# Two pads that move where the on-chip tiles of a decoder block begin

## The chip, the core and the metric

The kernel runs on one core of a Trainium2 chip. The metric is the device time of one execution in microseconds (us); the time before is the median of three runs, 918.95 us (918.89 to 918.98). Engines are named as in the profile: PE is TensorE's matmul side, PEld its weight loads, DVE is VectorE, ACT is ScalarE, POOL is GpSimd, SP is the engine that issues most DMAs.

## What is computed

A decoder block on 512 tokens of width 1024, all in float32. Cut to its products:

```python
u = rmsnorm(x, norm_mix_g)
p = u @ w_in + b_in                      # 1024 -> 7424 columns, split in nine parts
y_attn = sliding_window_sink_attention(aq, ak, av, sinks)   # 16 heads, window 128
y_hgrn = hgrn2_branch(hq, hf, hi, hg, lb, hgrn_norm_g)      # 8 heads, chunks of 64
h = x + (sigmoid(gate_a) * (y_attn @ w_branch_attn)
         + sigmoid(gate_b) * (y_hgrn @ w_branch_hgrn)) @ w_out
u2 = rmsnorm(h, norm_ffn_g)
z = silu(u2 @ w_gate) * (u2 @ w_up)      # 2816 wide
out = rmsnorm(h + z @ w_down, norm_final_g)
```

## The kernel before, in words

[...] Each operand is split into a high part `h`, rounded to float32r, and a low part `l`, the rest; the three products hh, hl and lh are summed in PSUM. So a product of a 128-row block needs three matmuls, each with a weight load of its own.

Weights come from DRAM in units of 1 MB (`raw`, two buffers, class `Weights`), and are cut into granules of half a unit. ACT writes a granule's `wh` (L96) and DVE its `wl` (L100), 128 x 1024 each, three buffers of each, two granules ahead of use. A granule is used by 24 matmuls.

The stages, in the order of TensorE's work, which is the order of the program text:

- x is normalized, transposed and split into `uh` and `ul` (up to about 30 us).
- A stream of projections from `uh`, `ul` (`mm3`, L357 to L359, into `ps_big`: the weights are loaded into the array, 512 columns of `uh` or `ul` move). Attention per head group (`sc`, `pt`, `pv`) and then HGRN per head (`pa`, `pc`, `pk`, `pu`, `po`, `pot`) are put in between, in slots of 8 matmuls. The HGRN values (`ps_v`, `mm3n`, L367 to L369) have it the other way round: a block of `uh` is loaded, 256 columns of `wh` or `wl` move.
- The branch products: `ps_big` with `yh`, `yl` moving (attention's output, beside the last HGRN heads), and with `oh`, `ol` moving (HGRN's output), the latter in turn with four pairs of gate projections from `uh`, `ul`.
- The output projection (`ps_o`, `mm3n`): blocks of `mh`, `ml` are loaded, 256 columns of weights move.
- FFN gate and up (`ps_f`, `mm3`): weights are loaded, 512 columns of `u2h` or `u2l` move. POOL, ACT and DVE make `zh`, `zl` from it.
- Down projection (`acc`, L865): blocks of `zh`, `zl` are loaded, 512 columns of `wh` or `wl` move. Then the last rmsnorm and the stores.

On-chip memory has an address per partition. Pools stand on two stacks: pools of side "left" are put one above the other from the bottom, pools of side "right" one below the other from the top (`newpool`, L141). Where a pool begins thus follows from the sizes of those before it. The first on the left is `cst`, the constants, 8,896 bytes a partition, which begins at byte 16,512; `w`, with the weight buffers, begins right above it. On the right nothing stands below the first pool's top at byte 229,344. The bytes at which the operands of the matmuls begin, as the program places them:

| tiles | side | first byte | modulo 512 |
|---|---|---|---|
| `raw`, `wh`, `wl` (all buffers) | left | 25,408 to 62,272 | 320 |
| `uh`, `ul` | left | 66,368, 82,752 | 320 |
| `u2h`, `u2l` | left | 82,752, 101,184 | 320 |
| `zh`, `zl` | right | 139,232, 184,288 | 480 |
| `oh`, `ol` | right | 151,520, 167,904 | 480 |
| `yh` and `mh`, `yl` and `ml` | right | 196,576, 212,960 | 480 |
| `khh`, `kll`, `qst` (attention) | right | 116,384 and up | 160 |
| `ident` | left | 16,512 | 128 |

Slices of these tiles that one matmul reads begin a multiple of 512 bytes further on, so the last column holds for every matmul. The highest left tile that lives beside the lowest right tile, `m1` in the pool `gates`, ends at 115,520; `khh0` begins at 116,384, 864 bytes above it. Later pools use again what earlier ones of the other side left free: `of`, `u2l` and `diag` on the left, and attention tiles, `zg`, `sgf`, `gfin` and `yo` on the right, share bytes in this way.

Of the kernel before, what the change touches and what calls it, by code (L numbers as in the profile page):

```python
"""Hybrid decoder block: sliding-window GQA attention with sinks, HGRN2 gated
linear recurrence, sigmoid-gated merge, SwiGLU FFN, final rmsnorm.

Every product with a weight matrix runs in single-pass fp32r: an operand is
split exactly into h (rounded to fp32r) and l = x - h, and the products hh, hl
and lh are summed in fp32 in PSUM.
"""
# [1 line left out]

# [6 lines left out]
F32 = mybir.dt.float32  # L16
# [6 lines left out]
P = 128  # L23
# [11 lines left out]
WARM = 28  # L35
AHEAD = 2


class Weights:
    """Streams weights: 1 MB units from DRAM, cut into granules split in h, l."""  # L40

    def __init__(self, nc, pool, units):
        self.nc, self.pool = nc, pool
# [22 lines left out]
        self.raw[u] = t  # L66

    def load_half(self, u, half):
        """A column half of a unit of kind c, for an early start."""
        kind, w, c0 = self.units[u]  # L70
        if u not in self.raw:
            self.raw[u] = self.pool.tile([P, 2048], F32, tag="raw", bufs=2, name=f"raw{u}")
        self.nc.sync.dma_start(
            self.raw[u].rearrange("p (k n) -> p k n", k=KD)[:, :, half * P:half * P + P],
            w[:, c0 + half * P:c0 + half * P + P].rearrange("(k p) n -> p k n", p=P))
# [38 lines left out]
def block_kernel(ctx: ExitStack, tc: tile.TileContext, x, norm_mix_g, w_in, b_in,  # L114
# [6 lines left out]
    def raw_ins(ins):  # L121
        return getattr(ins, "ins", ins)

    def act(out_, in_, func, **kw):
        """An activation; those that need a table keep the order given here."""
        if func not in (AF.Sigmoid, AF.Exp, AF.Ln):
            return nc.scalar.activation(out_, in_, func, **kw)
        if tables["last"] is None:
            ins = nc.scalar.activation(out_, in_, func, **kw)
        else:  # L130
            with tc.issue_after(tables["last"]):
                ins = nc.scalar.activation(out_, in_, func, **kw)  # L132
        tables["last"] = raw_ins(ins)
        return ins
# [6 lines left out]
    def newpool(name, side, space=None):  # L141
        kw = dict(space=space) if space is not None else {}
        kw["reuse_waits"] = "tile"
        return tc.alloc_tile_pool(name=name, bufs=1, side=side, **kw)

# [1 line left out]
    units = [("c", w_in, C_K), ("c", w_in, 0)]  # L147
    for p in range(1, 4):
        units += [("c", w_in, 256 * p), ("c", w_in, C_GA + 256 * (p - 1))]
# [14 lines left out]
    units += [("f", w_d, 2 * p) for p in range(NF // 2)]  # L164

    cst = newpool("cst", "left")
    wpool = newpool("w", "left")
    upool = newpool("u", "left")
    W = Weights(nc, wpool, units)

# [1 line left out]
    ident = cst.tile([P, P], F32, name="ident")  # L172
    make_identity(nc, ident)
    ones = cst.tile([P, P], F32, name="ones")
# [12 lines left out]
    low_m = low.bitcast(U32).unsqueeze(1).broadcast_to([P, NT, P])  # L187
    up_m = up.bitcast(U32).unsqueeze(1).broadcast_to([P, NT, P])

# [1 line left out]
    spool = newpool("start", "right")  # L191
    psum = newpool("ps", "left", bass.MemoryType.PSUM)

# [6 lines left out]
    def psb(shape, name):  # L200
        return psum.tile(shape, F32, tag="big", bufs=3, name=name)

    xt = spool.tile([P, NT, D], F32, name="xt")
    rows = spool.tile([90, P], F32, name="rows")
# [21 lines left out]
    sinks = cst.tile([P, 16], F32, name="sinks")  # L226
# [1 line left out]
    hib = cst.tile([P, D], F32, name="hib")  # L228
    nc.sync.dma_start(hib, b_in[0:1, C_HI:C_HI + D].broadcast_to([P, D]))

    # the tensor engine's clock is released by activity: keep it busy till x is there
    pg = psb([P, P], "pg")
    for _ in range(WARM):
        pe.transpose(pg, ident, ident)
# [93 lines left out]
    yh = ypool.tile([P, KD, S], F32R, tag="h", name="yh")  # L328
    yl = ypool.tile([P, KD, S], F32R, tag="l", name="yl")

    # lower bounds: softmax over the two rows of logits, first row
    lb = cst.tile([P, 8], F32, name="lb")
    omlb = cst.tile([P, 8], F32, name="omlb")
    nhfb = cst.tile([P, 8], F32, name="nhfb")
# [15 lines left out]
    def bias(col):  # L350
        return prm[:, col // P:col // P + 1]

# [1 line left out]
    def mm3(ps, wh, wl, ah, al):  # L354
        """ps = w^T a, w stationary."""
        for k in range(KD):
            pe.matmul(ps, wh[:, k, :], ah[:, k, :], start=k == 0, stop=False)  # L357
            pe.matmul(ps, wh[:, k, :], al[:, k, :], start=False, stop=False)  # L358
            pe.matmul(ps, wl[:, k, :], ah[:, k, :], start=False, stop=k == KD - 1)  # L359
            if k in (2, 5):  # L360
                yield

    def mm3n(ps, ah, al, t, wh, wl, k0, first, last):
        """ps (+)= a[:, t]^T w over 4 K-blocks, a stationary."""
        ts = slice(t * P, (t + 1) * P)
        for k in range(4):
            pe.matmul(ps, ah[:, k0 + k, ts], wh[:, k, :], start=first and k == 0, stop=False)  # L367
            pe.matmul(ps, ah[:, k0 + k, ts], wl[:, k, :], start=False, stop=False)  # L368
            pe.matmul(ps, al[:, k0 + k, ts], wh[:, k, :], start=False,  # L369
                      stop=last and k == 3)  # L370
# [5 lines left out]
        evac(ps)  # L376
        yield

# [1 line left out]
    khh = [ap.tile([P, S], F32R, name=f"khh{g}") for g in range(2)]  # L380
    kll = [ap.tile([P, S], F32R, name=f"kll{g}") for g in range(2)]
    vhl = [ap.tile([P, NT, P], F32R, name=f"vhl{g}") for g in range(2)]
# [118 lines left out]
            act(yh[:, ks, :], yq, AF.Copy)  # L501
            tt(yl[:, ks, :], yq, yh.bitcast(F32)[:, ks, :], ALU.subtract)

# [1 line left out]
    pools = {}  # L505

    def open_hgrn():
# [8 lines left out]
    def v8(z):  # L516
        return z.rearrange("p (n c) -> p n c", c=64)

    def v42(z):
        return z.rearrange("p (s two c) -> p s two c", two=2, c=64)  # L520
# [4 lines left out]
    def T(tag, shape=(P, S), bufs=1, pool=None):  # L525
        return (pool or pools["h"]).tile(list(shape), F32, tag=tag, bufs=bufs, name=tag)
# [44 lines left out]
    def hgrn_prep(hd):  # L571
        z = hd_state[hd]
        sn, g, q = z["sn"], z["lf"], z["q"]
        om = omlb[:, hd:hd + 1]
        b = g
        dve.tensor_tensor_scan(b, reset, g, 0.0, ALU.mult, ALU.add)
        b8 = v8(b)
        d = T("d")
        tt(v8(d), b8, b8[:, :, 31:32].broadcast_to([P, 8, 64]), ALU.subtract)
        e = T("e", bufs=2)  # L580
        tt(v8(e), b8[:, :, 63:64].broadcast_to([P, 8, 64]), b8, ALU.subtract)
        E1, E2 = T("E1", bufs=2), T("E2", bufs=2)
        act(E1, d, AF.Exp)
        act(E2, d, AF.Exp, scale=-1.0)
        act(e, e, AF.Exp)
        EB = b
        act(EB, b, AF.Exp)
        dec = T("dec", (P, 8), 2)
        dve.tensor_copy(dec, v8(EB)[:, :, 63])
        dec2 = T("dec2", (P, NT), 2)  # L590
        d42 = dec.rearrange("p (s two) -> p s two", two=2)
        tt(dec2, d42[:, :, 0], d42[:, :, 1], ALU.mult)
        tt(E1, q, E1, ALU.mult)
        stt(E2, sn, om, E2, ALU.mult, ALU.mult)
        # intra-chunk on the diagonal, chunk 1 against chunk 0 of a pair beside it
        K0 = T("K0", (P, NT, 64), 2)
        QE1 = T("QE1", (P, NT, 64), 2)
        KS, QS = e, EB
        stt(K0, v42(sn)[:, :, 0, :], om, v42(e)[:, :, 0, :], ALU.mult, ALU.mult)
        stt(v42(KS)[:, :, 1, :], v42(sn)[:, :, 1, :], om, v42(e)[:, :, 1, :],  # L600
            ALU.mult, ALU.mult)
        tt(v42(KS)[:, :, 0, :], K0, d42[:, :, 1:2].broadcast_to([P, NT, 64]), ALU.mult)
        tt(QE1, v42(q)[:, :, 1, :], v42(EB)[:, :, 1, :], ALU.mult)
        tt(v42(QS)[:, :, 0, :], v42(q)[:, :, 0, :], v42(EB)[:, :, 0, :], ALU.mult)
        tt(v42(QS)[:, :, 1, :], QE1, d42[:, :, 0:1].broadcast_to([P, NT, 64]), ALU.mult)
        z.update(E1=E1, E2=E2, K0=K0, QE1=QE1, KS=KS, QS=QS, dec2=dec2)
# [40 lines left out]
    def hgrn_outputs(hd):  # L647
        z = hd_state[hd]
        A = pools["aT"][hd % 2]
        po = ps1([P, NT, P], "po")  # L650
        for s in range(NT):
            pe.matmul(po[:, s, :], A[:, s, :], z["v"][:, s, :], start=True, stop=s == 0)  # L652
            if s:
                pe.matmul(po[:, s, :], z["QS"][:, s * P:(s + 1) * P], z["st"][:, s - 1, :],
                          start=False, stop=True)
        # rmsnorm over the head's values
        sq = z["sq"] = T("sq", (P, NT, P))
        act(sq, po, AF.Square)
        ss4, r4 = T("ss4", (P, NT), 2), T("r4", (P, NT), 2)
        dve.tensor_reduce(ss4, sq, AX.X, ALU.add)  # L660
        rms_scale(r4, ss4, P, ss4)
        tt(sq, po, r4.unsqueeze(2).broadcast_to([P, NT, P]), ALU.mult)
# [6 lines left out]
        stt(pools["of"][:, hd, :], pt.rearrange("p s c -> p (s c)"), g_hn[:, hd:hd + 1],  # L669
            z["sg"], ALU.mult, ALU.mult)  # L670

# [1 line left out]
    def evac_ya(j):  # L673
        def go(ps):
            tt(m1[:, j, :], ps, m1[:, j, :], ALU.mult)
# [21 lines left out]
    beside = {}  # L697
# [31 lines left out]
    h1.release()  # L729
    h0.release()  # L730

# [1 line left out]
    mp = newpool("m", "right")  # L733
    ohlp = newpool("ohl", "right")
    oh = ohlp.tile([P, KD, S], F32R, name="oh")
# [38 lines left out]
    gpool.release()  # L774
    upool.release()

# [1 line left out]
    hpool = newpool("hn", "left")  # L778
    u2pool = newpool("u2", "left")
    rp = newpool("r", "right")  # L780
# [31 lines left out]
    rp.release()  # L812
    ypool.release()

# [1 line left out]
    zpool = newpool("z", "right")  # L816
    fp = newpool("f", "right")
    zh = zpool.tile([P, NF, S], F32R, name="zh")
# [10 lines left out]
    for p in range(NF // 2):  # L829
        gs = []  # L830
        for a in range(2):
            zg = fp.tile([P, S], F32, tag="zg", bufs=2, name="zg")
            first = p == 0 and a == 0
# [13 lines left out]
    fp.release()  # L847
    u2pool.release()

# [1 line left out]
    wd = newpool("wd", "left")  # L851
    dp = newpool("d", "right")
    gfin = dp.tile([P, D], F32, name="gfin")
# [19 lines left out]
    first = len(W.grans) - TAIL_F  # L873
    for i in range(first, len(W.grans)):
        W.split(i, wd, TAIL_F)
    for t in range(NT):
# [29 lines left out]
        stt(y[:, S + 256:D], y[:, S + 256:D], r1, gfin[:, S + 256:D], ALU.mult, ALU.mult)  # L906
        for q, hs in ((nc.scalar, slice(0, S)), (nc.sync, slice(S, D))):
            q.dma_start(out2[t * P:(t + 1) * P, hs], y[:, hs])
    for pl in (dp, zpool):
        pl.release()  # L910
    for pl in (wd, hpool, wpool, cst):
        pl.release()
# [31 lines left out]
```

## Time and profile before

| | |
|---|---|
| median of three runs | 918.95 us |
| span of the profiled execution | 917.3 us |
| instructions in the span | 11601 |
| PE busy | 905.9 us, 99% |
| PEld busy | 770.1 us, 84% |
| DVE, ACT, POOL busy | 463.2, 371.1, 142.8 us |
| HBM traffic | 82.90 MB read, 2.10 MB written |

The span runs from the first to the last instruction of the profiled execution; the device time holds the launch and the end around it too. A matmul's duration in the profile runs from its start to the modelled end of its drain, and two or three matmuls overlap; so durations of matmuls don't add up to time. The step from one start to the next does. In the timeline the first column is the start in us.

### The profile page before, as it was taken

To read this page: it belongs to the slowest core of one execution; us is meant where nothing else is said; L and a number is where in the kernel's file an instruction comes from. 1 tells how busy PE (TensorE), PEld (TensorE's weight loads), DVE (VectorE), ACT (ScalarE), POOL (GpSimd) and SP (SyncE) were. 2 spreads that over 40 slices of the span, in tenths; PEclk is the share of its full clock that TensorE was granted. 3 is DMA by queue.
4 is the path that set the end of the run, shared out by engine and by line. 5 is a ranking of instruction groups with operands and counts; after the bars stand their busy time and mean duration, and the time that the engine had idled before them with its cause. 6 is when DMAs were issued, how large, how long until landed. Compare 5 with 4: busy or idle time off the path is not lost.

```text
span 917.3 us, 11601 instructions
## 1 busy us (share of the span) xinstructions
PE 905.9 (99%) x4668; PEld 770.1 (84%) x4668; DVE 463.2 (50%) x725; ACT 371.1 (40%) x634; POOL 142.8 (16%) x148
## 2 busy tenths in 40 slices
PE   8999999999999999999999999999999999999996
PEld 7988889898888988888888998888888888888885
DVE  5677877647484855645345444344433443322314
ACT  5566765655452636125332443233222322211214
POOL 3004533300000000000000003222332233000004
PEclk9999999999999999999999999999999999999999
DMA  8231211323222141322252322222233332322212
GB/s 255 93 93 46 93 47 46 93 91 94 90 92 57 38 137 46 108 76 93 92 179 96 93 92 92 92 93 92 91 97 110 112 96 91 115 92 92 91 46 93
DMA packets 73522, 85.74 MB, mean 93 GB/s; under 512 B 1690, under 2 KB 68348, under 8 KB 73468
## 3 DMA queue, kind: packets, MB, share of 16 engines
q1 hardware_dynamic: 72876, 83.95, 28.7%
q10 hardware_dynamic: 592, 1.05, 0.3%
q8 instruction: 37, 0.61, 0.3%
q14 instruction: 17, 0.14, 0.0%
HBM read 82.90 MB, written 2.10 MB: 93 GB/s over the span
## 4 chain that ended last, share of the span: by engine, by line
PE 97%; SPq 1%; DMA 0%; POOL 0%; DVE 0%; issue 0%; ACT 0%; POOLq 0%; DVEq 0%
PE acc L865 13%; PE ps_big L358 13%; PE ps_big L359 13%; PE ps_big L357 13%; PE ps_f L357 9%; PE ps_f L359 9%; PE ps_f L358 9%; PE ps_o L367 2%; PE ps_o L369 2%; PE ps_o L368 2%; PE ps_v L368 2%; PE ps_v L369 2%; PE ps_v L367 2%; PE pv L493 1%; PE sc L437 1%; PE po L652 1%
## 5 line engine op out<-in xcount | busy, mean ns | idle before, releaser
L96 ACT ACTIVATE wh<-raw 128x1024 fp32r<-128x1024 f32 x147 | 155.2, 1059 | 400.9 <-PE ps_f L358 161.7
L100 DVE TENSOR_TENSOR wl<-raw,wh 128x1024 fp32r<-128x1024 f32 x147 | 180.3, 1228 | 163.4 <-ACT wh L96 162.4
L357 PE MATMUL ps_big<-uh,wh 128*128 128x512 f32 x376 | 148.7, 395 | 0.0
L358 PE MATMUL ps_big<-ul,wh 128*128 128x512 f32 x376 | 147.9, 393 | 0.0
L359 PE MATMUL ps_big<-uh,wl 128*128 128x512 f32 x376 | 147.8, 393 | 0.0
L358 PE MATMUL ps_f<-u2l,wh 128*128 128x512 f32 x352 | 137.2, 390 | 0.0
L359 PE MATMUL ps_f<-u2h,wl 128*128 128x512 f32 x352 | 136.9, 389 | 0.0
L357 PE MATMUL ps_f<-u2h,wh 128*128 128x512 f32 x352 | 136.8, 390 | 0.0
L359 PEld LDWEIGHTS ps_big<-uh,wl 128*128 128x128 f32 x376 | 70.7, 188 | 14.1
L358 PEld LDWEIGHTS ps_big<-ul,wh 128*128 128x128 f32 x376 | 70.7, 188 | 13.7
L357 PEld LDWEIGHTS ps_big<-uh,wh 128*128 128x128 f32 x376 | 70.7, 188 | 13.7
L359 PEld LDWEIGHTS ps_f<-u2h,wl 128*128 128x128 f32 x352 | 66.1, 188 | 14.0 <-issue 0.2
L358 PEld LDWEIGHTS ps_f<-u2l,wh 128*128 128x128 f32 x352 | 66.1, 188 | 13.9 <-issue 0.2
L357 PEld LDWEIGHTS ps_f<-u2h,wh 128*128 128x128 f32 x352 | 66.1, 188 | 13.5
L838 POOL TENSOR_TENSOR zg<-zg,sgf 128x512 f32<-128x512 f32 x22 | 39.4, 1794 | 160.9 <-ACT sgf L132 160.9
L865 PE MATMUL acc<-wh,zl 128*128 128x512 f32 x176 | 58.1, 395 | 0.0
L865 PE MATMUL acc<-wh,zh 128*128 128x512 f32 x176 | 58.0, 396 | 0.0
L865 PE MATMUL acc<-wl,zh 128*128 128x512 f32 x176 | 57.9, 394 | 0.0
L844 DVE TENSOR_TENSOR zz<-ps_f,zg 128x512 f32<-128x512 f32 x22 | 15.2, 691 | 62.6 <-PE ps_f L359 61.4
L243 POOL TENSOR_TENSOR r<-ss,neghalf 128x4 f32<-128x4 f32 x8 | 10.1, 1260 | 234.3 <-DVE ss L242 234.3
L834 DVE TENSOR_TENSOR zg<-ps_f,R 128x512 f32<-128x512 f32 x22 | 15.1, 691 | 62.2 <-PE ps_f L359 62.2
L865 PEld LDWEIGHTS acc<-wh,zh 128*128 128x128 f32 x176 | 33.0, 188 | 8.2
(222 smaller groups left out, 1560.6 us busy)
## 6 DMA issues: line engine op xcount, KB each, us to landing
raw<-in_w_in_dram SPq DMA_DIRECT2D x27, 1024.0 KB, 5.5
raw<-in_w_ffn_gate_dram SPq DMA_DIRECT2D x11, 1024.0 KB, 5.3
raw<-in_w_ffn_up_dram SPq DMA_DIRECT2D x11, 1024.0 KB, 5.3
raw<-in_w_ffn_down_dram SPq DMA_DIRECT2D x11, 1024.0 KB, 4.9
raw<-in_w_branch_attn_dram SPq DMA_DIRECT2D x4, 1024.0 KB, 6.0
raw<-in_w_branch_hgrn_dram SPq DMA_DIRECT2D x4, 1024.0 KB, 5.2
raw<-in_w_out_dram SPq DMA_DIRECT2D x4, 1024.0 KB, 5.9
xt<-in_x_dram SPq DMA_DIRECT2D x4, 512.0 KB, 7.3
```

Source lines behind the costliest of these rows:

```text
L96: nc.scalar.activation(hv, src, AF.Copy)
L100: (low or nc.vector).tensor_tensor(lv, src, hv.bitcast(F32), ALU.subtract)
L357: pe.matmul(ps, wh[:, k, :], ah[:, k, :], start=k == 0, stop=False)
L358: pe.matmul(ps, wh[:, k, :], al[:, k, :], start=False, stop=False)
L359: pe.matmul(ps, wl[:, k, :], ah[:, k, :], start=False, stop=k == KD - 1)
L367: pe.matmul(ps, ah[:, k0 + k, ts], wh[:, k, :], start=first and k == 0, stop=False)
L368: pe.matmul(ps, ah[:, k0 + k, ts], wl[:, k, :], start=False, stop=False)
L369: pe.matmul(ps, al[:, k0 + k, ts], wh[:, k, :], start=False, stop=last and k == 3)
L834: tt(zg, fproject((lambda: row_broadcast(R, rstd2, u2pool)) if first else None), R, ALU.mult)
L838: pool_e.tensor_tensor(zg, zg, sg, ALU.mult)
L844: tt(z, fproject(), gs[a], ALU.mult)
L865: pe.matmul(acc[t][half], ah[:, f, ts], wv[:, 0, half * S:half * S + S], start=f == 0 and ah is zh and wv is wh, stop=f == NF - 1 and ah i ...
```

## The change

Two tiles that nothing reads or writes are put in. One of 192 bytes a partition is the first tile of the pool `cst`, so that all left pools move up by 192 bytes and `w` begins at 25,600, a multiple of 512. One of 480 bytes a partition is alone in a new pool `top`, the first of the right side, so that all right pools move down by 480 bytes, below 228,864, a multiple of 512. `raw`, `wh`, `wl`, `uh`, `ul`, `u2h`, `u2l`, `zh`, `zl`, `oh`, `ol`, `yh`, `yl`, `mh` and `ml` then all begin at a multiple of 512; the attention tiles of the table are at 192 modulo 512, `ident` at 320. The rest of the diff takes out comments.

```diff
 ...
+CST_PAD, TOP_PAD = 192, 480
+
 ...
     cst = newpool("cst", "left")
+    cst.tile([P, CST_PAD // 4], F32, name="pad")
+    top = newpool("top", "right")
+    top.tile([P, TOP_PAD // 4], F32, name="toppad")
     wpool = newpool("w", "left")
 ...
-    for pl in (dp, zpool):
+    for pl in (dp, zpool, top):
         pl.release()
```

## Rows read from the trace of the kernel before

**Rows 1.** The page: span, engine shares, chain that ended last by engine.

```profile
span 917.3 us, 11601 instructions
PE 905.9 (99%) x4668; PEld 770.1 (84%) x4668; DVE 463.2 (50%) x725; ACT 371.1 (40%) x634; POOL 142.8 (16%) x148
...
PE 97%; SPq 1%; DMA 0%; POOL 0%; DVE 0%; issue 0%; ACT 0%; POOLq 0%; DVEq 0%
```

**Rows 2.** PE groups by form: count | busy us, mean ns of one | idle before.

```profile
L357 PE MATMUL ps_big<-uh,wh 128*128 128x512 f32 x376 | 148.7, 395 | 0.0
L358 PE MATMUL ps_big<-ul,wh 128*128 128x512 f32 x376 | 147.9, 393 | 0.0
...
L357 PE MATMUL ps_f<-u2h,wh 128*128 128x512 f32 x352 | 136.8, 390 | 0.0
L865 PE MATMUL acc<-wh,zl 128*128 128x512 f32 x176 | 58.1, 395 | 0.0
...
L367 PE MATMUL ps_o<-wh,mh 128*128 128x256 f32 x128 | 36.6, 286 | 0.0
L367 PE MATMUL ps_v<-wh,uh 128*128 128x256 f32 x128 | 36.5, 285 | 0.0
...
L357 PE MATMUL ps_big<-yh,wh 128*128 128x512 f32 x64 | 25.8, 403 | 0.0
...
L357 PE MATMUL ps_big<-oh,wh 128*128 128x512 f32 x64 | 25.4, 396 | 0.0
```

**Rows 3.** Timeline of PE (start us, duration us), FFN gate and up.

```profile
599.72 0.39 PE L359 MATMUL ps_f<-u2h,wl 128*128 128x512 f32 x1
...
601.99 0.39 PE L357 MATMUL ps_f<-u2h,wh 128*128 128x512 f32 x1
```

**Rows 4.** The timeline in the down projection, nine matmuls from first to last start.

```profile
807.73 0.39 PE L865 MATMUL acc<-wh,zl 128*128 128x512 f32 x1
807.96 0.63 PE L865 MATMUL acc<-wh,zh 128*128 128x512 f32 x2
...
809.83 0.39 PE L865 MATMUL acc<-wl,zh 128*128 128x512 f32 x1
```

**Rows 5.** The timeline where a gate projection ends and 48 HGRN branch products follow.

```profile
429.78 0.39 PE L358 MATMUL ps_big<-ul,wh 128*128 128x512 f32 x1
430.01 0.39 PE L359 MATMUL ps_big<-uh,wl 128*128 128x512 f32 x1
430.23 0.40 PE L357 MATMUL ps_big<-oh,wh 128*128 128x512 f32 x1
...
441.48 0.39 PE L357 MATMUL ps_big<-uh,wh 128*128 128x512 f32 x1
```

**Rows 6.** The timeline in the attention branch product, 18 matmuls between the starts.

```profile
365.73 0.40 PE L358 MATMUL ps_big<-yl,wh 128*128 128x512 f32 x1
...
369.95 0.39 PE L358 MATMUL ps_big<-yl,wh 128*128 128x512 f32 x1
```

**Rows 7.** The timeline in the output projection, 14 matmuls between the starts.

```profile
501.72 0.28 PE L367 MATMUL ps_o<-wh,mh 128*128 128x256 f32 x1
...
503.40 0.28 PE L369 MATMUL ps_o<-wh,ml 128*128 128x256 f32 x1
```

**Rows 8.** The timeline after a break by an HGRN head, eight matmuls between the last two.

```profile
286.92 0.48 PE L357 MATMUL ps_big<-uh,wh 128*128 128x512 f32 x1
287.23 0.40 PE L358 MATMUL ps_big<-ul,wh 128*128 128x512 f32 x1
...
289.09 0.60 PE L668 MATMUL pot<-ident,sq 128*128 128x128 f32 x4
```

**Rows 9.** Windows: PE, PEld, DVE, ACT, POOL busy us, PEclk, DMA share, GB/s.

```profile
560.00:660.00 100.00, 100.00 (x442) 82.81 (x442) 44.09 (x50) 31.23 (x40) 31.70 (x20) 1.00 0.34 105
...
800.00:840.00 40.00, 40.00 (x173) 32.17 (x172) 9.30 (x8) 7.44 (x7) 0.00 (x0) 1.00 0.23 79
```

**Rows 10.** DVE's groups by form, and DMA issues (KB, us to landing).

```profile
L100 DVE TENSOR_TENSOR wl<-raw,wh 128x1024 fp32r<-128x1024 f32 x147 | 180.3, 1228 | 163.4 <-ACT wh L96 162.4
...
raw<-in_w_ffn_down_dram SPq DMA_DIRECT2D x11, 1024.0 KB, 4.9
```

**Rows 11.** Windows, all engines: the start.

```profile
10.00:20.00 10.00, 7.98 (x62) 7.27 (x62) 6.36 (x16) 5.61 (x13) 4.27 (x5) 1.00 1.03 303
```

## Prediction

> **What bounds the kernel now.** I read the page's engine shares first: TensorE (PE) is busy 99% of a span of 917.3 us, and the chain that ended last is 97% PE [rows 1]. So the time is the sum of the steps from one matmul's start to the next, plus the start and the tail. Next come the PE groups by form. The five groups of 128x512 products do the same work, yet their mean duration runs from 390 to 403 ns [rows 2]. A duration includes the drain, so I then read the step itself, from start times in the timeline: first row of a run to last row, divided by the number of matmuls between. [...] What I find:
>
> - FFN gate and up (`ps_f`): 10 steps in 2.27 us, 227 ns [rows 3]. The count over 100 us agrees (442 matmuls, 226.2 ns) [rows 9].
> - Down projection (`acc`): 9 steps in 2.10 us, 233.3 ns [rows 4].
> - Branch product of the HGRN output (`oh`, `ol` moving): 48 steps in 11.25 us, 234.4 ns. The `uh` matmul just before it, with the same kind of weights, ends a run at 227 ns [rows 5].
> - Branch product of attention (`yh`, `yl` moving): 18 steps in 4.22 us, 234.4 ns [rows 6].
>
> Now the address table. In the 227 ns stretches both operands lie on the left side, both at 320 modulo 512. In the three stages of 233 and 234 ns one operand lies on the right at 480 and the other on the left at 320. 320 is a multiple of 64; 480 is a multiple of 32 only. The step of a matmul thus goes with where its operands start. Nothing else in these rows does: in the FFN window DVE, ACT and POOL are busy 44, 31 and 32 us of 100, in the down projection 9.3, 7.4 and 0 of 40 [rows 9], and it is the emptier stage that has the slower step.
>
> **The change part by part.** No instruction is added or removed, and the two pads are never written. The left side moves up by 192 bytes, the right side down by 480. The smallest free gap between the sides is 864 bytes, so 192 remain; by the table the same pairs of tiles overlap in time-shared memory before and after, so I cost waits at nothing. What is left is 4668 matmuls with other start addresses.
>
> 1. *Mixed pairs, 512 columns.* After the change left and right operands are both at 0 modulo 512: the same residue for both, and a multiple of 64, as in `ps_f`. I give them the `ps_f` step. `acc`: 528 x (233.3 - 226.7) = 3.5 us, all on the path, since PE is never idle there [rows 9]. `oh`, `ol`: 192 x (234.4 - 226.7) = 1.5 us. `yh`, `yl`: 192, but with HGRN work between them. After such a break left-left pairs do not run at 227 either: from 287.23 to 289.09 there are 8 steps of 232.5 ns [rows 8]. I take half the price, 3.8 ns, so 0.7 us; the ends are 0.4 (234.4 to 232.5) and 1.5.
> 2. *Mixed pairs, 256 columns* (`ps_o`, 384). 14 steps in 1.68 us are 120.0 ns [rows 7], and its durations (286) equal those of the left-left `ps_v` (285) [rows 2]. Here the mixing costs nothing, so nothing is won.
> 3. *Left-left pairs* (1128 of `ps_big`, 1056 of `ps_f`, 432 of `ps_v`). Both operands move by the same 192 bytes; their distance stays a multiple of 512, and 320 was already a multiple of 64. I take 0. No row shows an fp32r product that starts at a multiple of 128, so this is the unknown of the case. [...]
> 4. *Attention and HGRN tiles* go from 32 to 64 byte multiples, a few hundred short matmuls. Bounds: 0.5 us either way, taken as 0.
> 5. *DVE, ACT, DMA.* The split of a weight granule takes 1.228 us on DVE [rows 10], and its period is 24 steps, 5.44 us in the FFN: it stays hidden even if it became twice as long. The 1 MB weight loads land after 4.9 us [rows 10], two granules (10.9 us) ahead. Uncovered is only the start, where the DMA engines are full (share 1.03 from 10 to 20 us [rows 11]) and PE waits for x: a DMA 5% faster or slower there would be worth up to 0.5 us. Taken as 0.
>
> Sum: 3.5 + 1.5 + 0.7 = 5.7 us off the span, 917.3 to 911.6. The median is 918.95, so 1.65 us lie around the span: 913.2 us, 0.62% less. With the ends of items 1, 4 and 5 this case alone gives 911.4 to 914.6; with part of the 232.5 ns stretches after breaks coming down to 227 as well (1128 x at most 5 ns), as low as 907.
>
> **The rivals.**
>
> *No change.* The steps of 233 and 234 ns may belong to operands far apart in memory, one per side, not to the residue; the pads move neither to the other side. For it: `ps_o` is mixed and pays nothing, so the residue alone does not decide; and every stage of 233 or 234 ns does cross sides. Against: crossing sides alone does not cost `ps_o` anything either. Time 918.95, with the start and the small matmuls 918.4 to 919.5. [...]
>
> [...]
>
> *Slower.* The 227 ns step is a regular beat of moving stream and weight load that a break upsets [rows 8]. If that beat needs the present start (64 modulo 128) and a start at 0 gives the beat of the `oh` run in all groups, `ps_f` loses 1056 x 7.6 = 8.0 us and left-left `ps_big` 1128 x 3.4 = 3.8, while `acc` and `oh` gain nothing: 931 us. It decides once some 750 of the 2184 left-left products lose 7.6 ns, which outweighs the 5.7 us. Against it: both operands move together, so nothing in their relation changes.
>
> **How the numbers follow.** Forecast (mixed pairs gain, left-left stay): 0.50. Full or partial pace for all: 0.20. No change: 0.17. Slower: 0.13. About 0.2%, 1.8 us, is what a measurement can tell from no change. So faster 0.70, same 0.17, slower 0.13. The range holds the forecast and no change (0.67), and reaches down to the half gain of the second rival, 886, and up to about half of the loss, 926, some 0.14 more; the full gain at 856 and the full loss stay outside.
>
> **What would show it.** Steps in the timeline decide. `acc` and `oh` at 227 ns with `ps_f` still at 227: the forecast. [...] `acc` and `oh` unchanged: the first. `ps_f` above 227: the third. The prediction would also be wrong if DVE, ACT or DMA times moved enough to open gaps on PE, which would stand as idle time before its groups, now 0.0 [rows 2].

## The result and the profile after

The changed kernel takes 911.5 us (median of four runs, 911.25 to 911.83) against 918.92 us (918.88 to 918.98) for the kernel before on the same chip: a ratio of 0.9919 with a 95% interval of 0.9905 to 0.9933, 7.4 us or 0.8% less. The forecast was 913.2 us. Of all executions in this study one, of the first experiment, took 2338.7 us at a granted clock of 1.0; no run shows why, and the ratios leave it out.

The page of after: span, engine shares, and the engines of the chain that ended last, to be held against [rows 1].

```profile
span 910.0 us, 11601 instructions
PE 899.6 (99%) x4668; PEld 769.8 (85%) x4668; DVE 463.3 (51%) x725; ACT 371.0 (41%) x634; POOL 142.8 (16%) x148
...
PE 97%; SPq 1%; DMA 0%; POOL 0%; DVE 0%; issue 0%; ACT 0%; POOLq 0%; DVEq 0%
```

The same instructions in the same order, and PE is busy 99% of a span that is 7.3 us shorter. The other engines' busy times stand still. So matmuls became cheaper; nothing was hidden better. Which ones, the groups by form of after tell (count | busy us, mean ns of one | idle before), against [rows 2]:

```profile
L362 PE MATMUL ps_big<-uh,wh 128*128 128x512 f32 x376 | 148.8, 396 | 0.0
L362 PE MATMUL ps_f<-u2h,wh 128*128 128x512 f32 x352 | 136.8, 390 | 0.0
L870 PE MATMUL acc<-wh,zl 128*128 128x512 f32 x176 | 56.9, 389 | 0.0
L372 PE MATMUL ps_o<-wh,mh 128*128 128x256 f32 x128 | 36.7, 287 | 0.0
L372 PE MATMUL ps_v<-wh,uh 128*128 128x256 f32 x128 | 36.5, 285 | 0.0
L362 PE MATMUL ps_big<-yh,wh 128*128 128x512 f32 x64 | 25.4, 397 | 0.0
L362 PE MATMUL ps_big<-oh,wh 128*128 128x512 f32 x64 | 24.9, 389 | 0.0
```

The left-left groups, with both operands on the left side (`uh`, `u2h`, `ps_v`), and `ps_o` are within 1 ns of before. The mixed groups of 512 columns came down by 6 or 7 ns: `acc` 395 to 389, `oh` 396 to 389, `yh` 403 to 397. The step itself stands in PE's timeline of after (start us, duration us): first the down projection, 11 steps from first to last start, then the HGRN branch product, 48 steps.

```profile
799.70 0.39 PE L870 MATMUL acc<-wh,zh 128*128 128x512 f32 x1
...
802.19 0.39 PE L870 MATMUL acc<-wh,zh 128*128 128x512 f32 x1
```

```profile
427.99 0.39 PE L362 MATMUL ps_big<-oh,wh 128*128 128x512 f32 x1
...
438.87 0.39 PE L362 MATMUL ps_big<-uh,wh 128*128 128x512 f32 x1
```

2.49 us by 11 is 226 ns where [rows 4] had 233; 10.88 us by 48 is 226.7 where [rows 5] had 234.4. This is the step of `ps_f` [rows 3]. The steps of each group, start to start and summed over the whole trace, give the account (the start is taken up in the fifth experiment):

| group | before, us | after, us | difference | predicted |
|---|---|---|---|---|
| `acc` | 122.97 | 119.45 | -3.52 | -3.5 |
| `oh`, `ol` | 44.97 | 43.52 | -1.45 | -1.5 |
| `yh`, `yl` | 45.69 | 44.57 | -1.13 | -0.7 |
| `ps_f` | | | +0.01 | 0 |
| `ps_o` | | | -0.04 | 0 |
| left-left `ps_big` | | | -0.15 | 0 |
| attention and HGRN | | | -0.05 | 0 |
| start (up to the first projections) | | | -1.0 | 0 |
| span | 917.3 | 910.0 | -7.3 | -5.7 |

### The profile page after: what moved, and what is told of

Read it like the earlier page. It is cut to its first block, busy times and chain, and to the rows that moved or that the text cites. A ratio compares the mean times of both kernels' runs of the same rounds, so it can differ in the third digit from the quotient of the medians.

```text
span 910.0 us, 11601 instructions
## 1 busy us (share of the span) xinstructions
PE 899.6 (99%) x4668; PEld 769.8 (85%) x4668; DVE 463.3 (51%) x725; ACT 371.0 (41%) x634; POOL 142.8 (16%) x148
## 4 chain that ended last, share of the span: by engine, by line
PE 97%; SPq 1%; DMA 0%; POOL 0%; DVE 0%; issue 0%; ACT 0%; POOLq 0%; DVEq 0%
PE acc L870 13%; PE ps_big L362 13%; PE ps_big L363 13%; PE ps_big L364 13%; PE ps_f L364 9%; PE ps_f L363 9%; PE ps_f L362 9%; PE ps_o L374 2%; PE ps_v L373 2%; PE ps_o L373 2%; PE ps_o L372 2%; PE ps_v L374 2%; PE ps_v L372 2%; PE pv L498 1%; PE sc L442 1%; PE pa L619 1%
## 5 line engine op out<-in xcount | busy, mean ns | idle before, releaser
L363 PEld LDWEIGHTS ps_big<-ul,wh 128*128 128x128 f32 x376 | 70.8, 188 | 13.6
```

## The experiments

The size came out nearly right, but the reason given for it had two halves, "the same residue for both" and "a multiple of 64", and this change makes both true at once. The runs take them apart. The *distance* of a pair below is the first byte of the moving operand less that of the loaded one, modulo 512. Before, it was 160 for `oh` and `yh`, which move and lie right, and 352 for `acc` and `ps_o`, where the right tile is the loaded one; 0 for all left-left pairs.

For each run two windows of PE serve as a gauge: 600 to 700 us lies in gate and up (`ps_f`), 800 to 900 us in the down projection (`acc`). The columns are the stretch, its length and PE's busy time with the count of matmuls, the granted clock, the DMA share and GB/s. The count also holds the matmuls cut by the ends, about two, so the step is 100 us by the count less two: 443 means 226.8 ns, 430 means 233.6. Before:

```profile
600.00:700.00 100.00, 100.00 (x443) 1.00 0.32 100
800.00:900.00 100.00, 100.00 (x430) 1.00 0.23 77
```

After:

```profile
600.00:700.00 100.00, 100.00 (x443) 1.00 0.30 95
800.00:900.00 100.00, 100.00 (x443) 1.00 0.25 85
```

### Multiples of 64 at different residues

Only the right side moves, by 32 bytes, to 448 modulo 512; the left stays at 320. Both are multiples of 64; right is 128 above left.

```diff
-CST_PAD, TOP_PAD = 192, 480
+CST_PAD, TOP_PAD = 0, 32
-    cst.tile([P, CST_PAD // 4], F32, name="pad")
```

> Only the right side moves, by 32 bytes: right tiles from 480 to 448 modulo 512 (a multiple of 64), left tiles stay at 320. Theory A (an operand of a 512-column product pays about 7 ns where it begins off a multiple of 64): `acc` and `oh` steps fall to 227 ns, `ps_f` stays 227; the matmul part of the gain comes whole, 5.7 to 6.3 us. Rival B (512-byte starts, or the same residue modulo 512 on both sides, are needed): `acc` 233, `oh` 234, time as before, 918.9 us. Start: if the first microsecond won by the change comes from weight tiles on a multiple of 256 bytes, it is not won here (weights stay at 64 modulo 256), so A gives about 912.8; if it comes from elsewhere, 912.

Measured: 916.97 us against 918.99, ratio 0.9977 (0.9967 to 0.9986). The windows of this run:

```profile
600.00:700.00 100.00, 100.00 (x443) 1.00 0.33 103
800.00:900.00 100.00, 100.00 (x432) 1.00 0.23 79
```

`acc` steps by 232.4 ns, `oh` by 233.3, `yh` by 232.4. A start at a multiple of 64 on both sides is not enough; that half of the reason falls. The rival's 918.9 us isn't met either: the 2.0 us gained are spread thin (`acc` 0.5, left-left `ps_big` 0.5, `ps_o` 0.3, `yh` 0.3, `oh` 0.2). Why the steps of `ps_big` fell, whose operands stayed where they were, isn't shown.

### The same distance at other starts

Only the left side moves, by 32 bytes, to 352; the right stays at 480. Neither is a multiple of 64 now; right is again 128 above left.

```diff
-CST_PAD, TOP_PAD = 192, 480
+CST_PAD, TOP_PAD = 32, 0
-    top.tile([P, TOP_PAD // 4], F32, name="toppad")
```

> Only the left side moves, by 32 bytes: left tiles at 352, right at 480 modulo 512; both are 32 off a multiple of 64, their distance is a multiple of 64. Theory A1 (each operand's own start counts): now all operands are off, so `ps_f` and `uh` products go to 233 to 234 ns, `acc` and `oh` stay there or get worse; ps_f loses about 7.5 us and `uh` products 4 to 6, time 930 us or more. Rival A2 (only the distance between the two operands counts, modulo 64): `ps_f` stays 227, `acc` and `oh` fall to 227, about 913 us.

Measured: 917.02 us, ratio 0.9979 (0.997 to 0.9989). The windows:

```profile
600.00:700.00 100.00, 100.00 (x443) 1.00 0.33 103
800.00:900.00 100.00, 100.00 (x432) 1.00 0.23 79
```

They are those of the run before, and so are the steps of the product groups. Neither theory on record holds: `ps_f` doesn't rise, and `acc` and `oh` don't fall to 227 ns at a distance that is a multiple of 64. `ps_f` has 226.8 ns with both operands at 352, as at 320 and at 0. So where the operands begin doesn't matter; how far apart they begin does. With that the two rivals that hang on a start, full pace and slower, fall as well.

### The left side alone

The pad of `cst` stays, that of the right side goes: left at 0, right at 480, so that `oh` and `yh` have a distance of 480, `acc` and `ps_o` one of 32.

```diff
-CST_PAD, TOP_PAD = 192, 480
+CST_PAD, TOP_PAD = 192, 0
-    top.tile([P, TOP_PAD // 4], F32, name="toppad")
```

> The left pad alone: left tiles at 0, right tiles stay at 480 modulo 512. Theory A: `acc` 233 and `oh` 234 as before, no gain there, `ps_f` 227. The weight tiles are on a multiple of 256 bytes here: if that is what the loads at the start gain from, x of the second half is ready about 1 us earlier and the time is about 918; if the gain at the start comes from x on the right side or is chance, 918.9. Rival (absolute start of the weights decides for `acc` and `oh`): 913.

Measured: 916.06 us, ratio 0.997 (0.9959 to 0.9981). The windows, then one group by form of the output projection:

```profile
600.00:700.00 100.00, 100.00 (x443) 1.00 0.30 97
800.00:900.00 100.00, 100.00 (x431) 1.00 0.23 79
```

```profile
L371 PE MATMUL ps_o<-wh,mh 128*128 128x256 f32 x128 | 36.2, 283 | 0.0
```

`acc` stays at 233.3 ns and `oh` comes to 233.4, so the mixed pairs of 512 columns gain next to nothing from the left pad alone. The start became 1.6 us shorter, where the expectation had about 1 us as one of two possibilities. And, not expected, `ps_o`, 256 columns, whose duration [rows 2] fell from 286 to 283 ns, went from 121.8 ns a step (a mean over all steps, waits included) to 118.8, 1.2 us in all: a size at which equal residues bring nothing, but 32 bytes of distance do.

### 32 bytes put between a left-left pair

In the changed kernel `u2h` and `u2l` are moved up by 32 bytes. Nothing else differs; `ps_f` has both operands on the left, as always.

```diff
     u2pool = newpool("u2", "left")
+    u2pool.tile([P, 8], F32, name="u2pad")
```

> The changed kernel with 32 bytes more ahead of `u2h`, so that `u2h`, `R`, `u2l` begin at 32 modulo 512 and everything else stays at 0. The cost that the change took from `oh` is put on `ps_f` alone, where the moving operand is then off and the weights are not. Theory A: `ps_f` goes from 227 to about 234 ns, 1056 x 7.5 = 7.9 us, so about 919.4 us; all other groups as in the changed kernel. Rival (the step belongs to the stage and to crossing sides, not to the residue): 911.5 us.

Measured: 918.36 us, ratio 0.9994 (0.9985 to 1.0003): nearly the whole gain is gone. The windows, then the group of `ps_f` by form:

```profile
600.00:700.00 100.00, 100.00 (x430) 1.00 0.29 92
800.00:900.00 100.00, 100.00 (x443) 1.00 0.25 86
```

```profile
L362 PE MATMUL ps_f<-u2h,wh 128*128 128x512 f32 x352 | 138.9, 396 | 0.0
```

The two windows have changed places. `ps_f` goes from 226.8 to 233.3 ns a step, 6.9 us in all, while `acc`, `oh` and `yh` keep what they gained. The price follows the distance into a stage that the change under study didn't touch, on one side of memory, and has the size that it has across the sides. Of all runs this one shows it most directly.

### The start: the first weights

The 1.0 us at the start was put at 0 in the forecast. What waits there is DVE, in the timeline of DVE, before and then after (start us, duration us, in brackets the wait in us and what ended it):

```profile
17.06 0.17 DVE L319 TENSOR_SCALAR sink<-sinks 128x16 f32<-128x16 f32 x1 [2.06 <-DMA sinks<-in_attn_sinks_dram]
```

```profile
16.03 0.17 DVE L324 TENSOR_SCALAR sink<-sinks 128x16 f32<-128x16 f32 x1 [1.09 <-DMA sinks<-in_attn_sinks_dram]
```

DVE stands at an 8 KB load, `sinks`, which comes in behind the first weights, and the scaling of the second half of x is queued behind that. SP issues this load at 13.36 us before and at 12.63 us after, so 0.7 us of the gain are there before it begins; it is the issues ahead of it that end earlier. PE's transposes of x follow 1.03 and 1.04 us later, in the timeline of PE, before and after:

```profile
18.09 1.06 PE L271 MATMUL xs<-ident,xt 128*128 128x128 f32 x8 [0.76 <-DVE xt L260]
```

```profile
17.07 1.06 PE L276 MATMUL xs<-ident,xt 128*128 128x128 f32 x8 [0.35 <-DVE xt L265]
```

The four first weight loads, 512 KB each, go in packets of 512 bytes; all 4,194 such packets of the trace take 30.8 ns on the mean before and 27.0 after. To see whether it is their place in memory, the pad is put behind `raw` instead of ahead of it: `raw` is at 320 again, all operands of float32r products with weights stay at 0. The constants, `sinks` among them, go back by 192 bytes with it.

```diff
-    cst.tile([P, CST_PAD // 4], F32, name="pad")
...
+    wpool.tile([P, CST_PAD // 4], F32, name="pad")
```

> The changed kernel with the left pad put behind the two `raw` buffers instead of ahead of the constants: `raw` begins at 320 modulo 512 again (64 off a multiple of 256), and every operand of a float32r matmul stays at 0. Theory R (the start of the kernel is quicker because the 512-byte packets of the first weight loads land on a multiple of 256): the mean 512-byte packet is 30.8 ns again instead of 27.0, the wait for `sinks` on DVE ends near 17.1 us instead of 16.0, and the time is 1.0 to 1.6 us above the changed kernel, about 912.8 us. Rival (chance or `xt` on the right): packets may change, the time stays 911.5.

Beside it ran the changed kernel as it is:

> The changed kernel once more, beside the others of this call on the same chip: 911.5 us by every theory; the gain at the start, if it is the packets, is there again (wait for `sinks` ending near 16.0 us or earlier).

Measured: 912.76 us (912.68 to 913.03) with `raw` at 320, 911.41 us (911.37 to 911.58) as changed. The timelines of DVE and of PE with `raw` at 320:

```profile
17.13 0.17 DVE L324 TENSOR_SCALAR sink<-sinks 128x16 f32<-128x16 f32 x1 [2.26 <-DMA sinks<-in_attn_sinks_dram]
```

```profile
18.17 1.06 PE L276 MATMUL xs<-ident,xt 128*128 128x128 f32 x8 [0.88 <-DVE xt L265]
```

The packets are back at 30.9 ns and the start is that of before, within 0.1 us, with every product group as after. That it is `raw` and not the constants that counts is told by the packets, nearly all of which carry weights into `raw`. So 1.35 us of the gain are DMA, not TensorE: 4,194 packets x 3.9 ns over 16 engines is 1.0 us; the rest is no more than the spread of the start, since DVE's wait ended at 16.03 and at 15.77 us in two traces of the changed kernel.

### The distances in between

Three kernels put a distance of its own on each stage, by pads or by slices that begin a few elements into a longer tile. They have one run each, and are read by their steps alone. The first:

```diff
+    ypp = newpool("yp", "right")
+    ypp.tile([P, 16], F32, name="ypad")
...
+    ohp.tile([P, 48], F32, name="ohpad")
...
+    u2pool.tile([P, 64], F32, name="u2pad")
...
+    zpp.tile([P, 16], F32, name="zpad")
```

> The changed kernel with pads that give each stage another distance (moving operand minus loaded operand, modulo 512): `ps_f` 256, `acc` 64, `oh` 256, `yh` 448, `ps_o` 64. Theory D (only the distance counts, and only 0 modulo 512 gives the 227 ns step): `ps_f` 233 or so (+6.5 us), `acc` 232 to 233 (+3.3), `oh` 233 to 234, `yh` 234; about 923 us. Rival D256 (0 modulo 256 is enough): `ps_f` and `oh` stay 227, `acc` 233; about 915.5. Rival D64 (a multiple of 64 is enough) is already against the 128-byte distances of the runs before: all 227, 911.5.

Measured: 912.26 us. `ps_f` at a distance of 256 has 226.8 ns, `oh` at 256 has 226.7. So the distance counts modulo 256, not 512. `acc` at 64 has 228.9, `yh` at 448 (192 modulo 256) 233.3. The windows show the first and the third:

```profile
600.00:700.00 100.00, 100.00 (x443) 1.00 0.30 95
800.00:900.00 100.00, 100.00 (x439) 1.00 0.25 85
```

The second sets `acc` to 256, `oh` to 320, `yh` to 384, and `ps_f` to 16 bytes:

```diff
+    ypp.tile([P, 32], F32, name="ypad")
+    ohp.tile([P, 16], F32, name="ohpad")
+    zpp.tile([P, 64], F32, name="zpad")
+    u2h = u2pool.tile([P, KD * S + 128], F32R, name="u2h")[:, 4:4 + KD * S].rearrange("p (k s) -> p k s", k=KD)
```

> As the run before, other distances: `ps_f` 16 (inside a 32-byte block), `acc` 256, `oh` 320, `yh` 384, `ps_o` 128. Theory D: all of them off the beat, 232 to 235 ns, about 923 us. Rival D256: `acc` stays 227. Rival D32 (only whole 32-byte blocks count): `ps_f` stays 227 at a distance of 16.

Measured: 917.21 us.

```profile
600.00:700.00 100.00, 100.00 (x433) 1.00 0.30 94
800.00:900.00 100.00, 100.00 (x443) 1.00 0.25 85
```

`acc` at 256 is at 226.8 again; `ps_f` at 16 pays 231.7; `oh` at 320, which is 64, has 229.2 on the mean, and `yh` at 384, which is 128, 232.4. The third goes down to 8 and up to 240 (496):

```diff
+    ypp.tile([P, 40], F32, name="ypad")
+    u2h = u2pool.tile([P, KD * S + 128], F32R, name="u2h")[:, 2:2 + KD * S].rearrange("p (k s) -> p k s", k=KD)
+    zh = zpool.tile([P, NF * S + 128], F32R, name="zh")[:, 4:4 + NF * S].rearrange("p (k s) -> p k s", k=NF)
```

> As the two kernels with distances by stage: `ps_f` 8 (two columns), `acc` 496 (240 modulo 256), `yh` and `oh` 352 (96 modulo 256), `ps_o` 160. Theory D256 (only 0 modulo 256 runs at 227 ns): `ps_f` 230 to 232 (+4 us), `acc` 231 to 233, `oh` 233 to 234. Rival (a few bytes do not matter, since the reads go by larger blocks): `ps_f` and `acc` 227.

Measured: 925.11 us, slower than before. Of the 13.6 us above the changed kernel about 12 are matmul steps (`ps_f` 6.9, `acc` 3.5, `oh` 1.3, `yh` 1.0, less 0.5 in `ps_o`). Another 1.4 are at the start, whose operands lie as in the changed kernel: in this one execution the granted clock was at 0.50 from 12.47 to 15.88 us, after PE had waited 1.83 us for `uh` up to 11.45; the other traces have 1.00 there. The first window is 10 to 20 us of this run, with PE, PEld, DVE, ACT and POOL ahead of the clock, the other two are as before.

```profile
10.00:20.00 10.00, 8.53 (x57) 8.33 (x58) 7.45 (x16) 6.02 (x13) 4.26 (x5) 0.83 0.94 294
```

```profile
600.00:700.00 100.00, 100.00 (x430) 1.00 0.29 95
800.00:900.00 100.00, 100.00 (x430) 1.00 0.25 84
```

8 bytes cost as much as 160: `ps_f` has 233.3, `acc` 233.3, `yh` and `oh` 233.5. All runs together, step by distance modulo 256 (for 512 columns the mean of the steps without a wait, for `ps_o` the mean of all):

| distance | 0 | 8 | 16 | 32 | 64 | 96 | 128 | 160 | 192 | 224 | 240 |
|---|---|---|---|---|---|---|---|---|---|---|---|
| 512 columns, ns | 226.7 | 233.3 | 231.7 | 233.3 | 229 | 233.3 | 232 to 233 | 234.2 | 233.3 | 233.4 | 233.3 |
| 256 columns (`ps_o`), ns | 121.8 | | | 118.8 | 119.8 | 121.8 | 121 | 120.4 | | | |

For 512 columns only 0 is free, with 64 a third of the way up. For 256 columns the order is another one: 0 is among the worst.

### Is there a version that beats the change?

By this table `ps_o` would be 1.2 us faster at 32. The whole right side is put at a distance of 256 and `mh` 32 bytes below that (`ml` likewise; `yh` and `yl`, which share their buffers, are sliced so that they stay at 256):

```diff
-CST_PAD, TOP_PAD = 192, 480
+CST_PAD, TOP_PAD = 192, 224
-    mh = ypool.tile([P, KD, S], F32R, tag="h", name="mh")
+    mh = ypool.tile([P, KD * S + 56], F32R, tag="h", name="mh")[:, 56:56 + KD * S].rearrange("p (k s) -> p k s", k=KD)
...
```

> The changed kernel with two things altered. The right pad is 224 instead of 480, so right tiles begin at a multiple of 256, not of 512, while left ones stay at 0: if a distance of 0 modulo 256 is the law, `acc`, `oh`, `yh` stay at 227 ns (rival, modulo 512: `acc` 233, +3.5 us). And `mh`, `ml` begin 32 bytes below a multiple of 256, so that the 256-column products of `ps_o` have the distance 32, which ran at 118.8 ns a step where the left pad stood alone: `ps_o` 45.6 instead of 46.75 us. Together 910.3 us; if the 118.8 came from elsewhere, 911.5.

Measured: 912.12 us, ratio 0.9924 (0.991 to 0.9937), so no better than the change. The trace, which is of the execution of 910.25 us, has what was expected: `acc` and `oh` at 226.7 ns and `yh` at 227.9 at a distance of 256, as in the changed kernel, and `ps_o` down from 46.8 to 45.6 us. The down projection:

```profile
800.00:900.00 100.00, 100.00 (x443) 1.00 0.25 85
```

But the five executions are 910.25, 910.88, 912.12, 912.2 and 912.43 us, the longer ones at a mean granted clock of 0.996 against 0.998 to 0.999. The kernel before has executions at 0.995 and 0.996 too, at most 0.7 us above its median, so this mean alone doesn't tell a longer time. A stretch at half clock like the one in the run with the distance of 8 bytes (3.4 us long, so an estimated 1.7 us lost) would have the size; but no long execution was traced, and why this kernel has them and the change had none isn't shown.

The other idea takes DVE's wait for `sinks` out of the way of x: the step that needs `sinks` is issued behind the scaling of x.

```diff
-    dve.tensor_scalar(sink8, sinks, 8.0, None, ALU.mult)
+    with tc.issue_after(scaled_x):
+        dve.tensor_scalar(sink8, sinks, 8.0, None, ALU.mult)
```

> The changed kernel with one DVE instruction (`sink8`, L324, which waits for the DMA of `sinks`) put behind the normalization of the second half of x; the two POOL copies that read it move too. Theory S (the gain at the start runs through this wait: DVE and POOL stand behind it): the 1.07 us that the wait still costs go, the transposes of the second half begin up to 1 us earlier, PE's idle time before them (0.35, 0.31 and 0.24 us) goes, 0.6 to 0.9 us, about 910.7. Rival (the second half of x is late anyway, by its own DMA): 911.4.

Measured: 911.04 us (910.86 to 911.31), ratio 0.9915 (0.9901 to 0.9928). DVE's timeline shows the new order, without a wait ahead of the scaling:

```profile
15.56 0.75 DVE L265 TENSOR_SCALAR xt<-xt,rstd 128x1024 f32<-128x1024 f32 x1
...
18.56 0.17 DVE L325 TENSOR_SCALAR sink<-sinks 128x16 f32<-128x16 f32 x1
```

The scaling starts at 15.56 us instead of 16.18. The median is some 0.4 us below that of the change, but the intervals of the two ratios overlap almost whole, so this isn't shown to be a gain. Both together:

> Both alterations of the two runs before in one kernel: they lie in different stages, so the gains add, 911.4 - 1.1 - 0.7 = 909.6 us.

Measured: 911.92 us (909.51 to 913.01), ratio 0.9916 (0.9903 to 0.9929). The shortest execution, 909.51, is the lowest time seen in the study, but the longer ones return, again at a mean clock of 0.996, and by the median nothing here is shown to beat the change.

## Why the prediction was right, and where its reason was not

*What bounds the kernel.* Right. PE's share and its chain are unchanged, and every microsecond of the difference is in matmul steps or ahead of the first of them.

*Item 1, mixed pairs of 512 columns.* Right in place and size: `acc` -3.52 for -3.5, `oh` -1.45 for -1.5. `yh` was mis-sized: -1.13 for -0.7. Half the price was taken because of the HGRN work in between; its steps without a wait came down from 234.3 to 227.9 ns on the mean, 6.4 of the 7.7 ns, so most of the price applies there; about a quarter of the steps stay above 228 ns.

*The reason behind item 1.* The address table gave the right pair of columns to compare, and "the same residue for both" is what decides (the second and the fourth experiment). "And a multiple of 64" is wrong: with both at multiples of 64 the price stays (`oh` 233.3 ns in the first experiment), and with neither the cheap step stays (`ps_f` 226.8 ns in the second). The residue that counts is modulo 256 (226.8 and 226.7 ns at a distance of 256); the change makes 512 equal, which is more than is needed. From the table of before alone the two halves couldn't be told apart, since all cheap pairs of 512 columns there have both.

*Items 2 to 4.* Right at 0: `ps_o` -0.04 us, `ps_f` +0.01, left-left `ps_big` -0.15, attention and HGRN -0.05. That `ps_o` gains nothing was read as "the mixing costs nothing". In fact its step does depend on the distance, by up to 3 ns, but 96 before and 0 after happen to cost the same 121.8.

*Item 5.* The term that was missed. The start was named as the only uncovered place and bounded at 0.5 us, from a DMA 5% faster. The packets of the first loads became 12% faster (30.8 to 27.0 ns), and the start gave 1.0 us in the profiled pair and 1.35 in the runs made for it. What it is in the place of `raw` that sets this isn't shown: at 352 modulo 512 (the second experiment) the packets took 30.8 ns as at 320, and those of 1,024 bytes went from 52.0 to 51.2 ns only, 1.5%.

*The sum.* 5.7 us predicted, 7.3 found in the spans: 1.0 at the start, 0.4 in `yh`, 0.2 spread over the rest.

*The rivals.* No change: falls, `acc` and `oh` run at the step of `ps_f` though their operands are still at the two ends of memory. Full pace (0.20 in the chances, 856 and 886 in the range): falls, `ps_f` with both operands at 0 modulo 512 keeps 226.8 ns. No run shows the shorter steps that these two times are worked out from; the lowest mean step of these products was 226.7 ns at 512 columns (distance 0) and 118.8 ns at 256 (`ps_o` at 32). Slower: falls for this change (its 3.4 ns for left-left `ps_big` are 234.4 less 231, an estimate: 227 ns [rows 3] and the 4 ns that its durations lie above those of `ps_f` [rows 2]; all steps of before, waits included, have a mean of 231.8); yet its picture, that the cheap step of left-left pairs can be upset and then costs 7 ns each, is what the fourth experiment did with 32 bytes, through the distance and not through the start.

What stays open is why the distance matters, and why 256 columns have another order than 512: no run here shows it.

## What to carry to other kernels

Where PE is the bound and groups of equal matmuls have different steps, list where the moving and the loaded operand begin, and compare their distance modulo 256 before anything else; a pad of some bytes set by it cost no instruction and gave 0.7% here. Choose by shape: in these fp32r products 512 columns wanted a distance of 0, 256 columns wanted 32 of the six distances tried. And where the start waits for DMA in small packets, let the tiles that it writes begin at a multiple of 512 bytes as well; here that was worth 1.0 to 1.4 us, with 512-byte packets.

## What the runs showed of the hardware that was not expected

- The step of an fp32r matmul of 512 columns with a weight load of its own depends on the distance of its two operands modulo 256 bytes: 226.7 ns at 0, 229 at 64, 231.7 to 234.2 at the nine other distances tried, 8 bytes among them. The start by itself makes no difference (`ps_f` has 226.8 ns at 0, 320 and 352 modulo 512); nor does the side: at 32 bytes `ps_f` (both left) and `acc` (one on each side) both have 233.3 ns, at 0 both 226.7 or 226.8.
- With 256 columns the order differs: 118.8 ns a step at 32, 121.8 at 0 and at 96.
- Packets of 512 bytes into on-chip memory took 27.0 ns at 0 modulo 512 and 30.8 at 320 and 352; those of 1,024 bytes hardly changed, 52.0 and 51.2.
- One 8 KB load, first in DVE's queue and issued behind the big ones, passed a DMA gain on to PE whole: DVE's wait for it ended 1.03 us earlier, and PE's transposes began 1.02 us earlier.
